# Softplus of the gates with tokens on partitions, and three feed-forward tiles split during the third branch's projection

## The chip, the cores and the metric

The kernel runs on one core of one Trainium2 chip. The metric is the device time of one execution in microseconds (us), taken as the median of several runs. The engines are TensorE (PE, matrix multiply; PEld is its weight load), VectorE (DVE), ScalarE (ACT), GpSimd (POOL) and SyncE (SP, which issues most DMAs).

## What is computed

Two layers of a hybrid decoder trunk on T = 288 tokens (256 of one prompt, 8 x 4 of eight decoding sequences), model width 1024, all in fp32. In each layer one projection feeds three mixers with four heads of width 128 each; their outputs are projected back, merged by sigmoid gates, and two layer norms follow, with a feed-forward block between them.

```
proj = einsum('btd,de->bte', x, w_in)
...
g = -exp(dn_A_log) * softplus(a_decay + dn_dt_bias)      # branch A, gated DeltaNet
gc = cumsum(g)                                           # in chunks
...
F = cumsum(log_sigmoid(m_f + ml_f_bias))                 # branch C, mLSTM
...
merged = g_a * (o_a @ w_br_a) + g_b * (o_b @ w_br_b) + g_c * (o_c @ w_br_c)
h = layer_norm(alpha * x + merged @ w_out, ln1_g, ln1_b)
ff = square(relu(h @ w_ff1)) @ w_ff2
out = layer_norm(alpha * h + ff, ln2_g, ln2_b)
```

Both `g` and `F` need a softplus (log_sigmoid(f) = -softplus(-f)) of four heads each, for every token: 8 x 288 numbers per layer.

## The kernel before, in words

Activations lie with channels on partitions and the 288 tokens in the free dimension. An fp32 product is made of three matmuls: the weights are split into `wh` (rounded) and `wl` (the rest), the activations into `XH` and `XL`, and `mm3` (L367 to L369) adds wh*XH, wh*XL and wl*XH. A full tile is 8 x 3 = 24 such matmuls of 128x288, and L498 is the same for tiles that fill gaps. `Stream.get` brings a weight tile: a 512 KB DMA on SP's queue into one of four `wr` buffers (L351), the cast to `wh` on ACT (L358), and the subtraction that gives `wl` on DVE (L360). With `get("B")` the two halves go to larger buffers, `bh` and `bl`, of a pool of 16, and so can be kept for longer.

A layer starts with the gates. Their projection is brought to 128 partitions by two small groups of matmuls, and ACT writes the biased gates `GT` (L626). Rows 32 to 35 are the forget gates of branch C, rows 64 to 67 the decay of branch A. Then the short convolutions of branch A (`conv_group`: ACT copies `CV` out of PSUM at L589 and L590, DVE builds `CO` at L604 and L607) go on beside the softplus, which works on all 128 partitions x 288 elements: U = GT*sgn (L643), E = exp(-|U|) on ACT (L645, L646), then a series in E/(2+E) on DVE (L648 to L659, with a RECIPROCAL at L649), U*sc (L660) and the running sum `CS` (scan, L662). From `CS` a chain of small operations on 4 partitions (L665 to L697) makes the running maximum and the row vectors `rc`, and at its end `drv` (L709 to L711) and `dr` (L714). PE's `dec` (L718), `colp` (L727) and `cols` (L737) take these up. The tiles of `rq`, `rk` and `rv` (branch B) are projected meanwhile; `rq` then goes through `rotary` (L570 to L572 on DVE).

Later in the layer, branch C's queries are scaled (`QL`, L1086), transposed on DVE (`Q`, L1090) and used by the matmuls `W` (L800). `ZG` (L542, L1022) gathers output gates.

After the mixers, `w_br_b`, `w_br_a` and `w_br_c` are applied in this order, in a loop over eight tiles `j` each; the merge into `mg` follows on DVE (L1301, L1302). The product with `w_out` (`wo`) feeds the generator `layer_norm`: per tile `yo` (L1343), sums `sd` and `sqs`; after the eighth tile the statistics `p` come back through PE, and a chain ACT, DVE (L1371 to L1380) makes `rstd`; `yo*rstd` (L1386) is split into `XH`, `XL` (L1388 to L1394), and the first feed-forward matmuls `f` (L375 to L377) begin. At the eighth `wo` tile (f = 8 of `AHEAD_FF`) the first five tiles of `w_ff1` are fetched with `get("B")`.

The build sets each engine's order from the dependencies and its own costs; `issue_after` in the source pins an instruction behind another one. All PSUM tiles come from two rings, `pm` (3) and `px` (5).

Of the kernel before, what the change touches and what calls it, by code (L numbers as in the profile page):

```python
# [9 lines left out]
F32 = mybir.dt.float32  # L10
# [13 lines left out]
GROUP = 3  # L24
# [226 lines left out]
def tile_trunk(ctx, tc, a):  # L251
# [36 lines left out]
    def R(name, dt=F32):  # L288
        return rp.tile([P, T], dt, tag="R", name=nm(name))
# [18 lines left out]
    for m_ in QM:  # L308
        G.memset(m_, 0.0)
    RB = cp.tile([P, T], F32R, name="RB")  # L310
# [8 lines left out]
    def C(n):  # L319
        o, s_ = CONST[n]  # L320
        return cst[:, o:o + s_]

    def VEC(l, n_, i, n=1):
        o = VECS[n_][0] + i
        return vec[:, l, o:o + n]
# [37 lines left out]

    def mm3(ps, hi, lo, xh, xl, start=True, stop=True):
        KT = len(xh)
        for k in range(KT):
            PE.matmul(ps, hi[:, k, :], xh[k], start=start and k == 0, stop=False)  # L367
            PE.matmul(ps, hi[:, k, :], xl[k], start=False, stop=False)  # L368
            PE.matmul(ps, lo[:, k, :], xh[k], start=False, stop=stop and k == KT - 1)  # L369
# [87 lines left out]
    for l in range(L):  # L457
# [168 lines left out]
        S.activation(GT, ps[:, :T], AF.Identity, bias=VEC(l, "gb", 0))  # L626

# [14 lines left out]
        U = R("U")  # L642
        V.tensor_scalar(U, GT, C("sgn"), None, op0=ALU.mult)  # L643
        E_ = R("E")
        S.activation(E_, U, AF.Abs)  # L645
        S.activation(E_, E_, AF.Exp, scale=-1.0)  # L646
        den = R("den")
# [3 lines left out]
        s2 = den  # L651
        V.tensor_tensor(s2, E_, E_, op=ALU.mult)
        pl = R("pl")
# [4 lines left out]
        V.tensor_scalar(U, U, 0.0, None, op0=ALU.max)  # L658
        V.scalar_tensor_tensor(U, pl, 2.0, U, op0=ALU.mult, op1=ALU.add)  # L659
        V.tensor_scalar(U, U, sc, None, op0=ALU.mult)  # L660
        CS = R("CS")
        V.tensor_tensor_scan(CS, C("rm"), U, 0.0, op0=ALU.mult, op1=ALU.add)  # L662
# [38 lines left out]
        rq = rotary(tproj("rq"))  # L701
# [572 lines left out]
        G.dma_start(a["o_m"][l], mo_[32:36, :])  # L1274

        MG_ = [h4(B("mg")) for _ in range(2)]
        for n_, (bi, wn) in enumerate(((1, "w_br_b"), (0, "w_br_a"), (2, "w_br_c"))):
# [14 lines left out]
            for j in range(8):  # L1292
                hi, lo = st.get()
                ps = PM("br")
                mm3(ps[:, :T], hi, lo, [OH[:, k, :] for k in range(4)], [OL[:, k, :] for k in range(4)])
                gt = TG[j // 4][:, j % 4, :]
# [139 lines left out]
        def prefetch_ff():  # L1436
            st = Stream([a["w_ff1"][l, i] for i in range(16)], 8)
            got = []

            def at(f):  # L1440
                n = AHEAD_FF[f]
                while len(got) < n:
                    got.append(st.get("B"))
                return got[:GROUP], (got[GROUP:], st)
            return at

# [82 lines left out]
```

## Time and profile before

| | before |
|---|---|
| median of 3 runs | 1219.05 us (1218.41 to 1221.0) |
| profiled execution, its own time | 1222.33 us |
| its span, first to last instruction | 1220.6 us |
| mean granted TensorE clock | 0.983 |
| busy: PE, PEld, DVE, ACT, POOL | 1178.3, 1146.9, 874.8, 639.1, 14.0 us |
| HBM read, written | 180.49 MB, 17.03 MB |

The profile gives one execution. Busy time is the time in which an engine had an instruction in work; "idle before" is the time an engine waited ahead of an instruction, with the one that released it. PEclk is the clock granted to TensorE, as a share of full speed (1.0 is 2.4 GHz, 0.5 is 1.2 GHz).

### The profile page before, as it was taken

The page shows a single profiled execution, that of the slowest core. Times are in us where ns is not written, and L with a number is a line of the kernel's source. Part 1 is how long each engine was busy: PE and PEld are TensorE (multiplying, and loading weights), DVE is VectorE, ACT ScalarE, POOL GpSimd, SP SyncE. Part 2 cuts the span into 40 slices and gives each one's busy share as a digit, 9 for nine tenths or more (in the row PEclk, how much of TensorE's full clock was granted, in tenths as well). Part 3 has the DMA queues.
Part 4 walks back from the last instruction along what each step waited for, and adds up shares of the span by engine and source line. Part 5 has one row for each costly group of instructions (what it writes and reads, how often), then busy time and mean ns, then how long its engine had stood idle before and what let it go on. Part 6 is the DMA issues. An engine that isn't in the chain of part 4 may idle for free.

```text
span 1220.6 us, 22885 instructions
## 1 busy us (share of the span) xinstructions
PE 1178.3 (97%) x9150; PEld 1146.9 (94%) x9150; DVE 874.8 (72%) x1655; ACT 639.1 (52%) x1162; POOL 14.0 (1%) x41
## 2 busy tenths in 40 slices
PE   8999999999999999999998998999999999999995
PEld 8899999999999899999998898999999989999995
DVE  5999856586668964566899995656866798545665
ACT  5745434883356653455584543349644566435542
POOL 1000000000000000000000000000000000000000
PEclk8999999999999999999999998999999999999998
DMA  8455635466655365555815354245666454555551
GB/s 304 128 157 134 232 91 164 136 243 207 222 155 171 97 185 169 168 162 161 257 40 179 123 187 143 96 139 213 229 200 193 146 172 133 162 170 163 166 156 39
DMA packets 69795, 201.15 MB, mean 165 GB/s; under 512 B 11688, under 2 KB 22232, under 8 KB 69560
## 3 DMA queue, kind: packets, MB, share of 16 engines
q1 hardware_dynamic: 68744, 197.51, 50.7%
q0 software_dynamic: 944, 2.17, 0.5%
q8 instruction: 72, 1.18, 0.4%
q14 instruction: 35, 0.29, 0.1%
HBM read 180.49 MB, written 17.03 MB: 162 GB/s over the span
## 4 chain that ended last, share of the span: by engine, by line
PE 81%; DVE 12%; ACT 3%; DMA 2%; issue 2%; SPq 0%; ACTq 0%; DVEq 0%
PE f L369 10%; PE f L368 10%; PE f L367 10%; PE pj L498 7%; PE pg L367 4%; PE pg L368 4%; PE pg L369 4%; PE pj L367 3%; PE pj L368 3%; PE pj L369 3%; DVE wl L360 3%; PE br L367 2%; PE br L368 2%; PE br L369 2%; DMA wr<-in_w_ff 2%
## 5 line engine op out<-in xcount | busy, mean ns | idle before, releaser
L358 ACT CAST wh<-wr 128x1024 fp32r<-128x1024 f32 x292 | 306.3, 1050 | 342.9 <-PE f L368 96.3
L360 DVE TENSOR_TENSOR wl<-wr,wh 128x1024 fp32r<-128x1024 f32 x292 | 356.1, 1223 | 173.6 <-ACT wh L358 173.0
L369 PE MATMUL f<-fh,wl 128*128 128x288 f32 x512 | 151.2, 295 | 0.0
L368 PE MATMUL f<-fl,wh 128*128 128x288 f32 x512 | 151.1, 295 | 0.0
L367 PE MATMUL f<-fh,wh 128*128 128x288 f32 x512 | 150.9, 295 | 0.0
L369 PE MATMUL f<-XH,wl 128*128 128x288 f32 x416 | 122.7, 295 | 0.7 <-DVE wl L360 0.7
L368 PE MATMUL f<-XL,wh 128*128 128x288 f32 x416 | 123.1, 296 | 0.0
L367 PE MATMUL f<-XH,wh 128*128 128x288 f32 x416 | 122.9, 296 | 0.0
L367 PE MATMUL pg<-XH,wh 128*128 128x288 f32 x384 | 114.2, 297 | 0.0
L368 PE MATMUL pg<-XL,wh 128*128 128x288 f32 x384 | 114.0, 297 | 0.0
L369 PE MATMUL pg<-XH,wl 128*128 128x288 f32 x384 | 113.4, 295 | 0.0
L369 PE MATMUL pj<-XH,wl 128*128 128x288 f32 x352 | 104.8, 300 | 3.4 <-DVE wl L360 3.4
L367 PE MATMUL pj<-XH,wh 128*128 128x288 f32 x352 | 106.1, 302 | 1.7 <-ACT CV L590 1.7
L368 PE MATMUL pj<-XL,wh 128*128 128x288 f32 x352 | 105.1, 299 | 0.0
L498 PE MATMUL pj<-XH,wh 128*128 128x288 f32 x320 | 98.2, 307 | 0.0
L498 PE MATMUL pj<-XH,wl 128*128 128x288 f32 x320 | 97.4, 305 | 0.3 <-DVE wl L360 0.3
L498 PE MATMUL pj<-XL,wh 128*128 128x288 f32 x320 | 97.0, 303 | 0.0
L367 PEld LDWEIGHTS f<-fh,wh 128*128 128x128 f32 x512 | 96.3, 188 | 0.2
L369 PEld LDWEIGHTS f<-fh,wl 128*128 128x128 f32 x512 | 96.2, 188 | 0.1
L368 PEld LDWEIGHTS f<-fl,wh 128*128 128x128 f32 x512 | 96.2, 188 | 0.1
L369 PEld LDWEIGHTS f<-XH,wl 128*128 128x128 f32 x416 | 78.5, 189 | 1.4 <-DVE wl L360 1.3
L367 PEld LDWEIGHTS f<-XH,wh 128*128 128x128 f32 x416 | 78.6, 189 | 0.0
(510 smaller groups left out, 2764.0 us busy)
## 6 DMA issues: line engine op xcount, KB each, us to landing
wr<-in_w_in SPq DMA_DIRECT2D x141, 512.0 KB
wr<-in_w_ff SPq DMA_DIRECT2D x128, 512.0 KB
wr<-in_w_out SPq DMA_DIRECT2D x16, 512.0 KB
S<-in_state_ml_C SPq DMA_DIRECT2D x8, 516.0 KB
S<-in_state_ret_R SPq DMA_DIRECT2D x8, 512.0 KB
out_s_R<-S SPq DMA_DIRECT2D x8, 512.0 KB
S<-in_state_dn_S SPq DMA_DIRECT2D x8, 512.0 KB
wr<-in_w_br_b SPq DMA_DIRECT2D x8, 512.0 KB
```

The costliest lines, as they stand in the source:

```text
L358: S.copy(hi[:, k, :], r[:, k, :])
L360: V.tensor_tensor(lo[:, k, :], r[:, k, :], hi[:, k, :].bitcast(F32), op=ALU.subtract)
L367: PE.matmul(ps, hi[:, k, :], xh[k], start=start and k == 0, stop=False)
L368: PE.matmul(ps, hi[:, k, :], xl[k], start=False, stop=False)
L369: PE.matmul(ps, lo[:, k, :], xh[k], start=False, stop=stop and k == KT - 1)
L498: ins = PE.matmul(self.ps[:, :T], self.w[i // 2][:, k, :], (xh, xl, xh)[i][k], start=self.k == 0, stop=self.k == 23)
```

## The change

Two edits, each in both layers.

**Softplus.** ACT now writes the sign-scaled gates U straight from PSUM, beside GT. Three PE transposes (`ut`) put the tokens on partitions, so that the eight gate rows that are needed become 3 x 2 x 4 = 24 elements on each of 128 partitions. The series runs on these 24 elements. Its last step writes into a zeroed tile `SPZ`, and three transposes (`sp`) bring the result back to 68 rows x 288. They are pinned behind the last matmul of `rq`, whose projection is now called ahead of them; U*sc and the scan work on 68 partitions.

**Feed-forward tiles.** The stream of `w_ff1` is made ahead of the merge loop, and three of its tiles are fetched in the third branch's loop, at j = 1, 3 and 5. Two are left for f = 8 of the layer norm.

```diff
--- before.py
+++ after.py
@@ -307,6 +307,8 @@
     QM = [cp.tile([P, H, T], F32, name=f"QM{i}") for i in range(2)]
     for m_ in QM:
         G.memset(m_, 0.0)
+    SPZ = cp.tile([P, 3, 68], F32, name="SPZ")
+    G.memset(SPZ, 0.0)
     RB = cp.tile([P, T], F32R, name="RB")
     V.memset(RB.bitcast(F32), 0.0)
     vec = cp.tile([P, L, VEC_W], F32, name="vec")
@@ -361,12 +363,14 @@
                 self.ready = [(hi[:, :, q:q + P], lo[:, :, q:q + P]) for q in range(0, sw, P)]
             return self.ready.pop(0)
 
+    mm_last = [None]
+
     def mm3(ps, hi, lo, xh, xl, start=True, stop=True):
         KT = len(xh)
         for k in range(KT):
             PE.matmul(ps, hi[:, k, :], xh[k], start=start and k == 0, stop=False)
             PE.matmul(ps, hi[:, k, :], xl[k], start=False, stop=False)
-            PE.matmul(ps, lo[:, k, :], xh[k], start=False, stop=stop and k == KT - 1)
+            mm_last[0] = PE.matmul(ps, lo[:, k, :], xh[k], start=False, stop=stop and k == KT - 1)
 
     def mm3_group(pss, tiles, xh, xl, ks=range(8)):
 
@@ -624,6 +628,9 @@
             PE.matmul(ps[32 * q:32 * q + 32, :T], C("gsel")[:, 4 * q:4 * q + 32], gp, start=True, stop=True,
                       tile_position=(0, 32 * q))
         S.activation(GT, ps[:, :T], AF.Identity, bias=VEC(l, "gb", 0))
+        sgb, U = K("sgb", 1), R("U")
+        V.tensor_tensor(sgb, VEC(l, "gb", 0), C("sgn"), op=ALU.mult)
+        S.activation(U, ps[:, :T], AF.Identity, bias=sgb, scale=C("sgn"))
 
         conv_group(1, "dk", None, dn_[:4])
         conv_group(2, "dv", st_dv, dn_[4:])
@@ -639,27 +646,35 @@
         G.memset(RS2, 0.0)
         S.activation(RS1[0:4], GT[0:4], AF.Tanh, scale=0.5)
         V.tensor_scalar(RS1[0:4], RS1[0:4], 0.5, 0.5, op0=ALU.mult, op1=ALU.add)
-        U = R("U")
-        V.tensor_scalar(U, GT, C("sgn"), None, op0=ALU.mult)
-        E_ = R("E")
-        S.activation(E_, U, AF.Abs)
+
+        ps = PX("ut")
+        for i, t0 in enumerate((0, P, T - P)):
+            PE.transpose(ps[:, i * P:(i + 1) * P], U[:, t0:t0 + P], ident)
+        u = ps[:, :3 * P].rearrange("p (c y x) -> p c y x", c=3, x=32)[:, :, 1:3, 0:4]
+        g3 = (lambda n_: K(n_, 3, 2, 4))
+        E_, den, pl, s2 = g3("gE"), g3("gden"), g3("gpl"), g3("gs2")
+        S.activation(E_, u, AF.Abs)
         S.activation(E_, E_, AF.Exp, scale=-1.0)
-        den = R("den")
         V.tensor_scalar(den, E_, 2.0, None, op0=ALU.add)
         V.reciprocal(den, den)
         V.tensor_tensor(E_, E_, den, op=ALU.mult)
-        s2 = den
         V.tensor_tensor(s2, E_, E_, op=ALU.mult)
-        pl = R("pl")
         V.tensor_scalar(pl, s2, 1.0 / 13, None, op0=ALU.mult)
         for d_ in (11, 9, 7, 5, 3):
             V.scalar_tensor_tensor(pl, pl, 1.0 / d_, s2, op0=ALU.add, op1=ALU.mult)
         V.scalar_tensor_tensor(pl, pl, 1.0, E_, op0=ALU.add, op1=ALU.mult)
-        V.tensor_scalar(U, U, 0.0, None, op0=ALU.max)
-        V.scalar_tensor_tensor(U, pl, 2.0, U, op0=ALU.mult, op1=ALU.add)
-        V.tensor_scalar(U, U, sc, None, op0=ALU.mult)
+        V.tensor_scalar(den, u, 0.0, None, op0=ALU.max)
+        for y in range(2):
+            V.scalar_tensor_tensor(SPZ[:, :, 32 + 32 * y:36 + 32 * y], pl[:, :, y, :], 2.0, den[:, :, y, :], op0=ALU.mult,
+                                   op1=ALU.add)
+        rq = tproj("rq")
+        ps = PX("sp")
+        with tc.issue_after(mm_last[0].ins):
+            for i, t0 in ((2, T - P), (1, P), (0, 0)):
+                PE.transpose(ps[:68, t0:t0 + P], SPZ[:, i, :], ident)
+        V.tensor_scalar(U[:68], ps[:68, :T], sc[:68], None, op0=ALU.mult)
         CS = R("CS")
-        V.tensor_tensor_scan(CS, C("rm"), U, 0.0, op0=ALU.mult, op1=ALU.add)
+        V.tensor_tensor_scan(CS[:68], C("rm")[:68], U[:68], 0.0, op0=ALU.mult, op1=ALU.add)
         Fr, gc = CS[32:36], CS[64:68]
         IT = R("IT")
         V.tensor_copy(IT[32:36], GT[96:100])
@@ -698,7 +713,7 @@
         for q in (0, 64):
             S.copy(RB[q:q + 4], rc_[q:q + 4])
             V.tensor_tensor(RB[q + 32:q + 36], rc_[q:q + 4], RB[q:q + 4].bitcast(F32), op=ALU.subtract)
-        rq = rotary(tproj("rq"))
+        rq = rotary(rq)
         rk, fill = tproj("rk", fill=True)
         rv, fill.then = tproj("rv", fill=True)
         fill.done = lambda: rotary(rk)
@@ -1272,6 +1287,15 @@
         fin_m = finish(OM, dn, MG, None, 2, 8, 9)
 
         G.dma_start(a["o_m"][l], mo_[32:36, :])
+        ff_st, ff_got = Stream([a["w_ff1"][l, i] for i in range(16)], 8), []
+
+        def prefetch_ff():
+            def at(f):
+                while len(ff_got) < AHEAD_FF[f]:
+                    ff_got.append(ff_st.get("B"))
+                return ff_got[:GROUP], (ff_got[GROUP:], ff_st)
+            return at
+
 
         MG_ = [h4(B("mg")) for _ in range(2)]
         for n_, (bi, wn) in enumerate(((1, "w_br_b"), (0, "w_br_a"), (2, "w_br_c"))):
@@ -1293,6 +1317,8 @@
                 hi, lo = st.get()
                 ps = PM("br")
                 mm3(ps[:, :T], hi, lo, [OH[:, k, :] for k in range(4)], [OL[:, k, :] for k in range(4)])
+                if n_ == 2 and j in (1, 3, 5):
+                    ff_got.append(ff_st.get("B"))
                 gt = TG[j // 4][:, j % 4, :]
                 mg = MG_[j // 4][:, j % 4, :]
                 if n_ == 0:
@@ -1433,17 +1459,6 @@
                                        op1=ALU.subtract)
             return [XF[:, f, :] for f in range(8)]
 
-        def prefetch_ff():
-            st = Stream([a["w_ff1"][l, i] for i in range(16)], 8)
-            got = []
-
-            def at(f):
-                n = AHEAD_FF[f]
-                while len(got) < n:
-                    got.append(st.get("B"))
-                return got[:GROUP], (got[GROUP:], st)
-            return at
-
         YO = [h4(B("yo")) for _ in range(2)]
         pre, (pre2, ff_st), ff_after = layer_norm(out_tiles(), YO, base_x, shift_x, "ln1_g", "ln1_b", prefetch_ff)
 
```

The order moves at three places on which the prediction rests. The numbers behind names count tiles; they differ between the two kernels for the same tile.

DVE, layer 0, around the `wl` of the first `rq` tile (before: `wl_714`; after: `wl_693`). `CO` is the convolution; `U`, `den`, `E`, `pl` are the softplus. Before:

```order
38 L604 SCALAR_TENSOR_TENSOR CO_626<-CV_487,vec,CO_626 128x312
39 L649 RECIPROCAL den_664<-den_664 128x288
40 L604 SCALAR_TENSOR_TENSOR CO_626<-CV_487,vec,CO_626 128x312 x2
41 L650 TENSOR_TENSOR E_661<-E_661,den_664 128x288
42 L604 SCALAR_TENSOR_TENSOR CO_626<-CV_487,vec,CO_626 128x312 x4
43 L652 TENSOR_TENSOR den_664<-E_661 128x288
44 L604 SCALAR_TENSOR_TENSOR CO_626<-CV_487,vec,CO_626 128x312
45 L654 TENSOR_SCALAR pl_669<-den_664 128x288
46 L360 TENSOR_TENSOR wl_714<-wr_711,wh_713 128x1024
```

After:

```order
33 L362 TENSOR_TENSOR wl_598<-wr_595,wh_597 128x1024
34 L608 SCALAR_TENSOR_TENSOR CO_632<-CV_493,vec,CO_632 128x312
35 L611 SCALAR_TENSOR_TENSOR CO_471<-CV_394,CO_471 128x1260
36 L608 SCALAR_TENSOR_TENSOR CO_632<-CV_493,vec,CO_632 128x312
37 L362 TENSOR_TENSOR wl_693<-wr_690,wh_692 128x1024
38 L608 SCALAR_TENSOR_TENSOR CO_632<-CV_493,vec,CO_632 128x312 x3
39 L362 TENSOR_TENSOR wl_725<-wr_722,wh_724 128x1024
40 L608 SCALAR_TENSOR_TENSOR CO_632<-CV_493,vec,CO_632 128x312 x4
41 L362 TENSOR_TENSOR wl_757<-wr_754,wh_756 128x1024
42 L608 SCALAR_TENSOR_TENSOR CO_632<-CV_493,vec,CO_632 128x312
43 L658 TENSOR_SCALAR gden_670<-gE_669 128x24
```

The `wl` of the first `rq` tile now stands ahead of all softplus operations but the 128x1 `sgb`, and two more of its tiles follow it there; the softplus comes behind the third.

DVE, layer 1, around `QL` and `Q` of branch C, for which PE's `W` waits. `ZG<-ZG,pj` takes a finished fill tile out of PSUM, `ZG<-tp,ZG` the result of eight transposes that PE does behind the last fill tile; `rst`, `rsu`, `fr` are 128x1. Before:

```order
1042 L391 TENSOR_SCALAR rsu_1334_8820<-rst_1333_8811 128x1
1043 L392 TENSOR_TENSOR rsu_1334_8820<-rsu_1334_8820,rst_1333_8811 128x1
1044 L542 SCALAR_TENSOR_TENSOR ZG_8680<-ZG_8680,pj_8765 128x288
1045 L1022 TENSOR_TENSOR ZG_8434<-tp_8792,ZG_8434 128x4x128
1046 L1022 TENSOR_TENSOR ZG_8434<-tp_8798,ZG_8434 128x4x128
1047 L393 SCALAR_TENSOR_TENSOR fr_1331_8809<-rsu_1334_8820,rsy_1332_8810 128x1
1048 L1086 TENSOR_TENSOR QL_8826<-qc_8318,cst 128x1152
1049 L1004 TENSOR_SCALAR fr_1331_8809<-fr_1331_8809 128x1
1050 L1090 STREAM_TRANSPOSE Q_1336_8828<-QL_8826 128x1152
```

After:

```order
1028 L546 SCALAR_TENSOR_TENSOR ZG_8706<-ZG_8706,pj_8714 128x288
1029 L996 SCALAR_TENSOR_TENSOR S_8559<-S_8559,up_8746 128x2x128
1030 L390 TENSOR_SCALAR rst_1341_8837<-rst_1341_8837 128x1
1031 L362 TENSOR_TENSOR wl_8865<-wr_8862,wh_8864 128x1024
1032 L391 TENSOR_TENSOR rsy_1340_8836<-rsy_1340_8836,rst_1341_8837 128x1
1033 L1101 TENSOR_TENSOR QL_8852<-qc_8344,cst 128x1152
1034 L546 SCALAR_TENSOR_TENSOR ZG_8706<-ZG_8706,pj_8758 128x288
1035 L392 TENSOR_TENSOR rst_1341_8837<-rsy_1340_8836 128x1
1036 L1105 STREAM_TRANSPOSE Q_1344_8854<-QL_8852 128x1152
```

`pj_8765` before is the last fill tile ahead of W; `pj_8758` after is the second last. QL and Q stand behind the last tile and the transposes before, and around the second-last tile after.

ACT, layer 0, at the end of the first layer norm. `wh<-wr` casts a weight tile that a DMA brings; `Cb<-sqs` and `Cb<-Cb` are the logarithm and exponential for `rstd`, and `sqt`, `XH<-yo` belong to the last tiles of `wo`. Before:

```order
337 L1345 ACTIVATE sqt_4730<-yo_4416 128x288
338 L333 ACTIVATE XH_4493<-yo_4416,vec 128x288
339 L358 CAST wh_4921<-wr_4919 128x1024
340 L1371 ACTIVATE Cb_4417<-p_726_4694 128x288
341 L358 CAST wh_5032<-wr_5030 128x1024
342 L358 CAST wh_5068<-wr_5066 128x1024
343 L1376 ACTIVATE Cb_4417<-sqs_4419 128x288
344 L1377 ACTIVATE Cb_4417<-Cb_4417 128x288
345 L1388 ACTIVATE XH_4493<-yo_4415,vec 128x288 x4
```

After:

```order
335 L360 CAST wh_4935<-wr_4933 128x1024
336 L1371 ACTIVATE sqt_4722<-yo_4448 128x288
337 L335 ACTIVATE XH_4525<-yo_4448,vec 128x288
338 L360 CAST wh_5046<-wr_5044 128x1024
339 L360 CAST wh_5082<-wr_5080 128x1024
340 L1371 ACTIVATE sqt_4762<-yo_4448 128x288
341 L335 ACTIVATE XH_4525<-yo_4448,vec 128x288
342 L1397 ACTIVATE Cb_4449<-p_739_4726 128x288
343 L1402 ACTIVATE Cb_4449<-sqs_4451 128x288
344 L1403 ACTIVATE Cb_4449<-Cb_4449 128x288
345 L1414 ACTIVATE XH_4525<-yo_4447,vec 128x288 x4
```

Two casts stood between the statistics `Cb<-p` and the logarithm; now all casts stand ahead of the statistics. On DVE, five `bl` splits stood among the operations on the last `wo` tiles, and two stand there now.

## Rows read from the trace of the kernel before

**Rows 1.** The page: busy time by engine.
```profile
PE 1178.3 (97%) x9150; PEld 1146.9 (94%) x9150; DVE 874.8 (72%) x1655; ACT 639.1 (52%) x1162; POOL 14.0 (1%) x41
```

**Rows 2.** PE's waits: who waited for whom, us in total, times, longest.
```profile
PE dec L718 <- DVE dr L714: 4.6, 2, 2.4
```

**Rows 3.** Windows: length, busy PE, PEld, DVE, ACT, POOL (instructions), PEclk, DMA share, GB/s.
```profile
40.00:50.00 10.00, 10.00 (x78) 10.00 (x77) 9.86 (x17) 8.26 (x19) 0.54 (x1) 1.00 0.57 184
50.00:60.00 10.00, 8.09 (x47) 7.63 (x46) 10.00 (x19) 4.50 (x10) 0.54 (x1) 0.83 0.29 81
650.00:660.00 10.00, 7.91 (x59) 7.68 (x59) 10.00 (x14) 4.19 (x7) 0.00 (x0) 1.00 0.49 161
740.00:750.00 10.00, 5.76 (x43) 5.56 (x42) 9.06 (x24) 2.70 (x4) 0.00 (x0) 0.92 0.72 262
344.00:356.00 12.00, 12.00 (x92) 12.00 (x92) 7.21 (x12) 5.81 (x11) 0.00 (x0) 1.00 0.56 158
356.00:368.00 12.00, 12.00 (x92) 11.94 (x91) 11.73 (x23) 5.82 (x10) 0.00 (x0) 1.00 0.43 146
```

**Rows 4.** Windows of stretches at half clock, the first and the last of six.
```profile
55.44:58.85 3.41, 3.41 (x17) 3.41 (x16) 3.41 (x6) 1.25 (x1) 0.00 (x0) 0.51 0.39 145
...
1007.90:1011.40 3.50, 3.50 (x17) 3.50 (x16) 3.50 (x11) 2.44 (x6) 0.00 (x0) 0.52 0.07 28
```

**Rows 5.** Timeline of PE, layer 0, first `rq` tile: start, us, instruction, [idle before].
```profile
52.66 0.40 PE L367 MATMUL pj<-XH,wh 128*128 128x288 f32 x1 [0.83 <-ACT CV L590]
...
54.27 0.40 PE L369 MATMUL pj<-XH,wl 128*128 128x288 f32 x1 [1.08 <-DVE wl L360]
```

**Rows 6.** DVE's groups by form, the whole execution: us in total, mean ns, idle before.
```profile
L649 DVE RECIPROCAL den<-den 128x288 f32<-128x288 f32 x2 | 3.9, 1946 | 0.0
L386 DVE TENSOR_SCALAR rst<-rst 128x9 f32<-128x9 f32 x4 | 0.7, 171 | 0.1
```

**Rows 7.** DVE's groups by form, 40 to 90 us (layer 0's gates).
```profile
L656 DVE SCALAR_TENSOR_TENSOR pl<-pl,den 128x288 f32<-128x288 f32 x5 | 2.2, 447 | 0.0
...
L571 DVE TENSOR_TENSOR rot<-rot,cst 128x1152 f32<-128x1152 f32 x1 | 1.4, 1352 | 0.0
```

**Rows 8.** Timeline of DVE, layer 0: the scan and the end of its chain.
```profile
64.93 0.76 DVE L662 TENSOR_TENSOR_SCAN CS<-cst,U 128x288 f32<-128x288 f32 x1
...
73.04 0.16 DVE L711 TENSOR_TENSOR drv<-vec,M 4x8 f32<-4x8 f32 x1
```

**Rows 9.** Timeline of PE and DVE, layer 1, ahead of `W`.
```profile
744.05 1.03 PE L1012 MATMUL tp<-ident,OR 128*128 128x128 f32 x8
745.15 1.28 DVE L1022 TENSOR_TENSOR ZG<-tp,ZG 128x512 f32<-128x512 f32 x2
746.41 1.35 DVE L1086 TENSOR_TENSOR QL<-qc,cst 128x1152 f32<-128x1152 f32 x1
747.80 1.38 DVE L1090 STREAM_TRANSPOSE Q<-QL 128x1152 f32<-128x1152 f32 x1
...
749.32 0.55 PE L800 MATMUL W<-Q,E 128*128 128x128 f32 x1 [4.24 <-DVE Q L1090]
```

**Rows 10.** Timeline of all engines, layer 0, end of the first layer norm.
```profile
396.39 1.22 DVE L360 TENSOR_TENSOR bl<-wr,bh 128x1024 fp32r<-128x1024 f32 x1
...
397.49 1.05 ACT L358 CAST wh<-wr 128x1024 fp32r<-128x1024 f32 x1 [0.49 <-DMA wr<-in_w_ff]
...
400.32 1.05 ACT L358 CAST wh<-wr 128x1024 fp32r<-128x1024 f32 x1 [1.78 <-DMA wr<-in_w_ff]
401.28 0.43 ACT L1376 ACTIVATE Cb<-sqs 128x288 f32<-128x288 f32 x1
...
405.02 0.82 DVE L1386 TENSOR_TENSOR yo<-yo,rstd 128x288 f32<-128x288 f32 x2
...
406.19 0.40 PE L375 MATMUL f<-XH,bh 128*128 128x288 f32 x1 [2.70 <-DVE XF L1392]
```

**Rows 11.** Timeline of PE, layer 1, first feed-forward matmuls.
```profile
1007.58 0.66 PE L375 MATMUL f<-XH,bh 128*128 128x288 f32 x2 [2.04 <-ACT XH L1388]
```

## Prediction, made before the changed kernel was run

> **What bounds the kernel now.** I read the busy times first: PE works 1178.3 of 1220.6 us and the next engine, DVE, 874.8 [rows 1]. So a change that takes no matmul away can only win the 42 us in which PE is idle, and the time that it loses at half clock. The mean granted clock of 0.983 says that the second is about half as large: 1.7% of the span is 20 us of lost clock.
>
> Next I read the list of PE's waits and looked each one up in the windows and the timeline. A full stretch holds 78 matmuls in 10 us, a pitch of 0.128 us (the stretch from 40 us, [rows 3]). At the head of `rq` in layer 0 the count is 47, and DVE is busy for all of the 10 us: 31 x 0.128 = 4.0 us are lost [rows 3]. PE stood there for a PSUM slot that ACT emptied late and then 1.08 us for the `wl` of the first `rq` tile [rows 5]; that `wl` was late because DVE took softplus and convolution operations ahead of it. In layer 1 the same place has 59 of 78, 2.4 us lost, again with DVE at 10.00 of 10 [rows 3]. Later PE waits 2.4 and 2.2 us for `dr`, the end of the gates' chain [rows 2], 4.24 us for `Q` in layer 1 [rows 9], 2.70 us at the end of the first layer norm in layer 0 and 2.04 us in layer 1 [rows 10, 11].
>
> What such a wait costs is more than its length. Behind five of these waits, and behind the pair at `rq`, the clock stands at about 0.5 for 3.4 to 3.9 us; PE had stood idle for 1 to 4 us just before [rows 4, 5, 9 to 11]. Seventeen matmuls fit in 3.41 us there, where 26 would at the full pitch: 1.2 us by the count, 1.7 by the clock. I take 1.5 us for each.
>
> **Part 1, the softplus.** On DVE it removes 14 operations of 128x288 per layer: the RECIPROCAL of 1.95 us [rows 6], nine with two tensor inputs at 0.45 us [rows 7], and four with one input, at two thirds of that: some 7 us. It adds a 128x1 product and 14 operations of 128x24 or less. None of that size stands in the trace. The bounds are 0.17 us (128x9, [rows 6]) and 0.45 us (128x288, [rows 7]); 24 elements are nearest to 9, so I take 0.18. For the small RECIPROCAL the bounds are 0.17 and 1.95; a twelfth of the long one's time above 0.17 gives 0.15 more, so 0.32. Together 14 x 0.18 + 0.32 = 2.8 us. DVE saves some 4.5 us (bounds 0.5 and 5) where it was busy without a break. Thirty-two times as many elements cost only 2.6 times as much [rows 6, 7]: that is why twelve times less work does not shrink twelvefold.
>
> ACT gets one more 128x288 write (about 0.45 us) and loses nearly as much on the two shorter ones; it is busy 4.5 of 10 us there [rows 3]. POOL's one memset lies at the program's start. Neither counts. PE gets six transposes per layer. Eight of PE's `tp` transposes take 1.03 us [rows 9], so these cost 0.8 us, all of it on the path.
>
> What matters more is the order. The three `wl` that `rq` needs first now stand ahead of the softplus on DVE, so the loss at the head of `rq` should go: 4.0 us in layer 0, 2.4 in layer 1.
>
> The end of the gates' chain I expect to gain nothing. The result now comes back through `sp`, which is held behind the 96 matmuls of `rq`. In layer 0 PE starts `rq` at 51.9 us after three transposes, ends it 96 x 0.129 = 12.4 us later at 64.3, and does `sp` until 64.7. U*sc and one `wl` (1.22 us, [rows 10]) stand ahead of the scan, which starts at about 66.4, where it was 64.93. From scan to `drv` took 8.1 us [rows 8], with one `wl` in it that is no longer there: 6.9, so 73.3. Behind `drv` DVE now does two of the rotary's long operations (1.35 us each, [rows 7]) and RB before `dr`: `dec` can go at 77.2, against 75.9 before. PE has 75 fill matmuls between `sp` and `dec` (it had 41 between `rq` and `dec`), and arrives at 64.7 + 75 x 0.129 = 74.4. So it waits 2.8 us where it waited 2.4, and the half clock stays. The balance at `dec` is 34 more matmuls done, 4.4 us, for 1.3 us later: **-3.1 us in layer 0**, transposes included. In layer 1 `dr` stood behind these two operations already. There I take the 2.4 us, less 0.8 for transposes, plus 0.4 because the chain has one `wl` less in it: **-2.0 us**.
>
> **The move of Q.** In layer 1 `QL` waited in DVE's order behind the last fill tile's `ZG` and two operations on transposes (1.28 us) that PE itself had only just made [rows 9]; then QL 1.35 and Q 1.38 followed, and W could go 4.24 us late. Now QL and Q stand around the second-last tile's `ZG`. That tile ends 24 x 0.129 = 3.1 us before the last one, and the eight transposes take 1.03: W is wanted 4.1 us behind the second-last tile, and 0.45 + 1.38 us with two 0.15 operations is what stands behind it on DVE, some 2.1 us. The wait of 4.24 and the 1.5 of half clock go, and I leave 0.5 for a late `ZG`: **-5.2 us**. In layer 0 no such wait exists to win.
>
> **Part 2, the feed-forward tiles.** At the end of the layer norm the logarithm stood on ACT behind a cast that waited 1.78 us for its DMA [rows 10], and three of the `bl` splits (1.22 us each) that stood between DVE's last operations are gone. Now the logarithm stands behind no cast, and `rstd`'s chain has no `wl` in its middle. The first `yo*rstd` was at 405.02; without 1.78 us of ACT's wait, one cast of 1.05 and one `wl` of 1.22 it comes 3 to 4 us sooner. PE had stood since 403.5 (406.19 less 2.70): the wait goes but for a few tenths. It is worth 2.70 + 1.5 = 4.2 us in layer 0 and 2.04 + 1.5 = 3.5 in layer 1. Of each I take four fifths, since other casts and splits move too: **-3.4 and -2.8 us**.
>
> The three tiles have to be split in the third branch's stretch instead. There DVE is busy 7.21 of 12 us and then 11.73 of 12, with PE full in both [rows 3]. Three splits are 3.7 us, three casts 3.2; the first stretch has 4.8 us free on DVE, the second none. The tiles come at j = 1, 3, 5, so two of them hit the full stretch, but `wl` buffers run a tile ahead. I cost it at nothing; the cover is the idle DVE before 356 us. If the cover is gone, each tile costs PE its 1.22 us: 3.7 us per layer plus 1.5 of clock. The DMAs move 146 GB/s of the 262 that another stretch shows [rows 3]; 1.5 MB more in 12 us makes 277, just at that mark.
>
> **The sum.** -3.1 - 2.0 - 5.2 - 3.4 - 2.8 = -16.5 us. Of this some 5.4 us are clock: 1.5 at `rq`, 1.5 at W, and four fifths of 1.5 at each layer norm. The profiled execution took 1222.33 us (its span is 1220.6), which makes 1205.8. It lies 3.3 us above the median of the runs, so against the median: 1219.05 - 16.5 = **1202.5 us**.
>
> On the clock the rows and a rule differ. The rows show a whole execution at 0.983, with a stretch at 0.51 behind each long wait [rows 4]. The Trainium skill (TensorE: Matmul & The Clock Gate, section What's actually happening) says that the loss while the clock comes up is under 1% of a typical kernel and should not be fitted for a model. By that rule the 5.4 us would be left out, and the estimate would be 1207.9 us. This trace loses 1.7%, in stretches that each have their wait, so I keep them.
>
> **The rivals.**
> 1. *Only the layer norm pays.* The wait moves: `dr` comes later by the rotary's 2.7 us in full, the gates' gain is spent at `dec`, and `Q` lands late again. For it speaks that DVE stays near full in these stretches; against it that `rq`'s `wl` and Q demonstrably move ahead in the order. It gives -6.2 and about -1: 1212.
> 2. *All of the waits go*, those for `dr` too, because DVE has 4.5 us less to do. Then the terms reach their full size (4.0 + 2.4 - 1.6 + 5.7 + 4.2 + 3.5 = 18.2) and 2.4 + 2.2 + 2 x 1.5 = 7.6 us come on top: 1193. Against it speaks `sp`'s place behind `rq`.
> 3. *Slower: the three early tiles starve the third branch.* A weight tile's DMA that came late held ACT, and casts followed each other at 2.8 us (397.49 to 400.32, [rows 10]). If the three tiles delay the tiles of `w_br_c` and `w_out` behind them on SP's queue and in the four `wr` buffers by that much each, PE loses 8.5 us and 1.5 to 3 of clock per layer, 21 in all: 1219.05 - 16.5 + 21 = 1224. It decides from 8.3 us per layer on. Against it: the DMA engines are 0.43 busy there [rows 3].
> 4. *No change.* PE has the same matmuls and twelve transposes more, 1.6 us; if each wait that goes comes back at the next place where DVE is full, the time is 1219 to 1221. Against it: behind the `rq` stretch, the W and the layer norm, the DVE has free time before PE next needs it. The Trainium skill (Perfetto Trace Analysis, section Identifying the Most-Contended Engine) says to optimize the engine with the highest occupancy first; by that rule, relieving DVE at 72% would win nothing, and this rival would be the forecast. The windows do not bear it out: in them DVE is the full engine and PE the one with gaps.
>
> **How the numbers follow.** Chances: the forecast 0.62, rival 1 0.17, rival 2 0.09, rival 3 0.06, rival 4 0.06. The range reaches from rival 2 to just past rival 1: 1193 to 1213, and leaves out rivals 3 and 4 and the tails. A change of 0.2% (2.4 us) is about what can be told from none. Faster by more: 0.88; within: 0.06; slower: 0.06.
>
> **What would show it.** PE's waits should no longer hold `W` on `Q`, `f` on `XF` or `XH`, or `pj` on `wl` at the head of `rq`; `dec` on `dr` should stay near 2 to 3 us in both layers. The count of matmuls in the first 10 us of `rq` should be above 70 in layer 0, and the mean clock rise towards 0.99. The small operations should take under 0.2 us, the RECIPROCAL under 0.4. It is wrong if W still waits, if PE waits in the third branch's loop or at `w_out`, or if `wo` waits grow by more than 3 us.

## The result, and the profile after

The changed kernel takes 1201.09 us (median of 4 runs, 1199.93 to 1203.68); the kernel before took 1218.73 us beside it. The ratio is 0.9861, with a 95% interval of 0.9842 to 0.9881: 17.6 us faster, against 16.5 forecast. Run again later beside other kernels it took 1200.16 us against 1219.86, a ratio of 0.9837 (0.9816 to 0.9859). The profiled execution took 1201.68 us, with a span of 1199.9 us.

The page's busy times, after:

```profile
PE 1170.1 (98%) x9162; PEld 1139.7 (95%) x9162; DVE 866.4 (72%) x1657; ACT 638.7 (53%) x1164; POOL 14.2 (1%) x42
```

PE's idle time fell from 42.3 us [rows 1] to 1199.9 - 1170.1 = 29.8. The mean granted clock rose from 0.983 to 0.992: lost clock went from 1.7% of 1220.6 us, 20.7, to 0.8% of 1199.9, 9.6. So 12.5 us of the gain in this pair are waits, and the rest comes out of the 11 us of clock. But the profiled execution of before had less clock than most: in the 17 runs of before beside the experiments below the median of the mean clock is 0.987, against 0.992 in the four runs of the changed kernel, which is about 6 us of clock and not 11. DVE's busy time fell by only 8.4 us, 4.2 per layer, where 4.5 was reckoned.

The list of PE's waits, after (who waited for whom, us in total, times, longest):

```profile
PE dec L733 <- DVE dr L729: 2.8, 2, 1.4
PE pj L502 <- ACT wh L360: 2.4, 2, 1.3
PE wo L371 <- DVE yo L1369: 1.7, 2, 0.9
...
PE cols L752 <- DVE rep L751: 1.2, 2, 0.7
```

No wait of `W` for `Q`, of `f` for `XF` or `XH`, or of `pj` for `wl` is left in the list, which answers to [rows 9 to 11] and [rows 5]. The largest that are left, `dec` and the `pj` ahead of it, stand at the end of the gates' chain.

The windows, after (length, busy PE, PEld, DVE, ACT, POOL with instructions, PEclk, DMA share, GB/s): the head of `rq` in layer 0, the end of the gates, `rq` in layer 1 from its head on (two that overlap), and two of the third branch.

```profile
50.00:60.00 10.00, 10.00 (x78) 10.00 (x77) 9.42 (x25) 6.49 (x15) 0.54 (x1) 1.00 0.57 164
70.00:80.00 10.00, 6.84 (x43) 6.04 (x43) 9.76 (x27) 3.97 (x8) 0.52 (x1) 0.86 0.03 10
640.00:650.00 10.00, 10.00 (x78) 10.00 (x77) 9.02 (x22) 6.79 (x13) 0.54 (x1) 1.00 0.53 166
645.00:655.00 10.00, 10.00 (x78) 9.98 (x77) 7.45 (x15) 5.50 (x8) 0.00 (x0) 1.00 0.51 157
344.00:356.00 12.00, 12.00 (x92) 12.00 (x92) 9.05 (x14) 7.39 (x11) 0.00 (x0) 1.00 0.87 268
356.00:368.00 12.00, 11.60 (x86) 11.13 (x85) 10.07 (x22) 5.19 (x10) 0.00 (x0) 1.00 0.45 143
```

At `rq` the counts are 78 where they were 47 and 59 [rows 3]. In the third branch the DMAs now move 268 GB/s where they moved 158, DVE is busy 9.05 of 12 us where it was 7.21, and PE loses 0.4 us in the second window, where `wo` begins.

DVE's groups by form, 45 to 66 us (layer 0's softplus):

```profile
L664 DVE SCALAR_TENSOR_TENSOR gpl<-gpl,gs 128x24 f32<-128x24 f32 x5 | 0.9, 180 | 0.1
...
L675 DVE TENSOR_SCALAR U<-sp,sc 68x288 f32<-68x288 f32 x1 | 0.5, 517 | 1.3 <-PE sp L674 1.3
L659 DVE RECIPROCAL gden<-gden 128x24 f32<-128x24 f32 x1 | 0.3, 296 | 0.0
```

A 24-element operation takes 0.18 us, as reckoned from the 9-element row [rows 6], and the RECIPROCAL 0.296, against 0.32. U*sc, which now reads the PSUM tile `sp`, takes 0.52 us; before it took 0.37 on 128x288, and I had left it at that. (That is four fifths of the 0.45 of a two-input operation, not the two thirds that I took for its kind; no term of the sum hangs on it.)

Where the time went is best read by laying the two traces side by side at the same matmul. Start of the first matmul of each kind, before and after, in the two profiled executions:

```
                         before    after   difference
last pj ahead of rq       51.00    49.77      -1.2
dec, layer 0              75.90    76.43      +0.5
sc (branch B's scores)   109.71   105.98      -3.7
W, layer 0               149.79   146.19      -3.6
wo, layer 0              363.95   360.37      -3.6
f, layer 0               406.19   400.52      -5.7
layer norm 2, layer 0    603.93   595.75      -8.2
sc, layer 1              707.65   695.58     -12.1
X (behind W), layer 1    762.00   745.31     -16.7
wo, layer 1              966.46   949.85     -16.6
f, layer 1              1007.58   989.35     -18.2
end of the span         1220.6   1199.9      -20.7
```

By stretches: ahead of `rq` -1.2, gates of layer 0 -2.5, first layer norm of layer 0 -4.6 with what follows it, gates of layer 1 -3.9, W -4.6, first layer norm of layer 1 -4.1 with the end of the program. The sum is the spans' 20.7 (rounding aside), 3 us more than the medians' difference: the profiled execution of before stood 3.3 us above the median of its runs, as the prediction said.

Three of these figures are not what they seem. Up to the last `pj` ahead of `rq` PE does the same in the same order in both kernels, so the first -1.2 does not come from the change; the clock at the program's start was lower for longer in the profiled execution of before. Its window from 5 to 16 us, and that of after:

```profile
5.00:16.00 11.00, 8.87 (x40) 8.11 (x41) 7.28 (x12) 6.93 (x11) 0.00 (x0) 0.69 1.03 356
5.00:16.00 11.00, 9.23 (x51) 8.46 (x51) 7.18 (x12) 6.91 (x12) 0.00 (x0) 0.84 1.03 358
```

And in layer 1 the two kernels do not do the same work between `sc` and W. The windows from the first `sc` to the first W, before and after:

```profile
707.65:749.32 41.67, 37.34 (x325) 34.12 (x324) 37.30 (x108) 18.52 (x31) 0.56 (x1) 0.99 0.62 215
695.58:735.48 39.90, 39.40 (x344) 36.61 (x343) 36.40 (x106) 17.21 (x32) 0.56 (x1) 1.00 0.59 197
```

Counted by their starts, 18 more matmuls of 128x288 stand there after the change, and 18 fewer ahead of `sc`: at 0.129 us each that is 2.3 us of work moved from the gates to W. With equal work the gates of layer 1 gained 3.9 - 2.3 = 1.6 us and W 4.6 + 2.3 = 6.9 us.

### The profile page after: what moved, and what is told of

Same layout as the page of the kernel before. It is cut to its first block, busy times and chain, and to the rows that moved or that the text cites. A ratio compares the mean times of both kernels' runs of the same rounds, so it can differ in the third digit from the quotient of the medians.

```text
span 1199.9 us, 22910 instructions
## 1 busy us (share of the span) xinstructions
PE 1170.1 (98%) x9162; PEld 1139.7 (95%) x9162; DVE 866.4 (72%) x1657; ACT 638.7 (53%) x1164; POOL 14.2 (1%) x42
## 4 chain that ended last, share of the span: by engine, by line
PE 89%; DVE 7%; ACT 1%; DMA 1%; issue 1%; SPq 0%; ACTq 0%; DVEq 0%
PE f L372 10%; PE f L371 10%; PE f L373 10%; PE pj L502 9%; PE pg L371 4%; PE pg L372 4%; PE pg L373 4%; PE pj L371 4%; PE pj L372 4%; PE pj L373 4%; PE br L371 2%; PE br L372 2%; PE br L373 2%; DVE wl L362 2%; PE tp L413 1%
```

## The experiments

Ten further kernels ran. The first four were compared with 17 runs of before (median 1219.47 us), the others with 17 more each time (1219.87 and 1219.86).

**The softplus edit alone.** The changed kernel without the early fetches:

```diff
-                if n_ == 2 and j in (1, 3, 5):
-                    ff_got.append(ff_st.get("B"))
```

> The softplus edit alone; all five feed-forward tiles are fetched at the end of the first layer norm as before. Theory: the two edits act in different stretches, and the place of Q and QL on DVE comes with this edit. From the two traces: 3.6 us gained by W of layer 0, 3.9 between the two layers' ends of the gates, 4.6 at W of layer 1, so about 12 us below before (some 1207 us), PE's waits for Q gone, and the 2.7 and 2.0 us waits for the first feed-forward matmuls still there. Rival: the time at W belongs to the other edit: then about 1212 us and W still waits 4 us for Q.

It took 1209.71 us, a ratio of 0.9925 (0.9903 to 0.9948): 9.8 us, where the two traces had made 12 expected. The first line of PE's list of waits:

```profile
PE f L379 <- ACT XH L1412: 4.4, 2, 2.4
```

The waits for the feed-forward's first matmuls are back, and in the list W has none. So what W gained belongs to this edit, which does not touch `Q` in the source: the build placed it elsewhere.

**The feed-forward edit alone**, on the kernel before:

```diff
+                if n_ == 2 and j in (1, 3, 5):
+                    ff_got.append(ff_st.get("B"))
```

> The feed-forward edit alone on the kernel before. Theory: the waits at the first feed-forward matmuls and the half clock behind them go in both layers, 4.6 + 4.0 us by the traces, so about 1210 to 1212 us; W still waits about 4 us for Q, the head of rq still loses 4.0 and 2.4 us. Rival: the three early splits cost PE time in the third branch (waits of wo or br above 1 us more per layer): then 1214 us or more.

It took 1211.90 us, a ratio of 0.9943 (0.9924 to 0.9962): 7.6 us. The two parts add up: 9.8 + 7.6 = 17.4, against 17.6 for both. Its list of waits begins with the three of before that are not the layer norm's:

```profile
PE dec L718 <- DVE dr L714: 4.6, 2, 2.4
PE W L800 <- DVE Q L1090: 4.2, 1, 4.2
PE pj L369 <- DVE wl L360: 3.4, 3, 2.1
```

**Q back behind the last fill tile.** The changed kernel, in layer 1:

```diff
-        V.tensor_tensor(QL...
+        with tc.issue_after(zg_last[0].ins) if l else nullcontext():
+            V.tensor_tensor(QL...
```

> The changed kernel, with QL of layer 1 pinned on DVE behind the last fill tile's ZG. Theory: the place of QL and Q on DVE is what the W term is made of: W waits again 2.5 to 4 us and the half clock comes back with it, so 3 to 5 us over the changed kernel (1204 to 1206 us). Rival: what W gained is lost or won elsewhere anyway: within 1 us of the changed kernel.

It took 1209.06 us, a ratio of 0.9923 (0.9899 to 0.9947): 8 us over the changed kernel, more than either theory said. The line of PE's waits, and then DVE ahead of W:

```profile
PE W L815 <- DVE Q L1106: 5.1, 1, 5.1
```

```profile
736.18 1.28 DVE L1037 TENSOR_TENSOR ZG<-tp,ZG 128x512 f32<-128x512 f32 x2
737.38 1.35 DVE L1102 TENSOR_TENSOR QL<-qc,cst 128x1152 f32<-128x1152 f32 x1
738.65 1.22 DVE L362 TENSOR_TENSOR wl<-wr,wh 128x1024 fp32r<-128x1024 f32 x1
739.78 1.37 DVE L1106 STREAM_TRANSPOSE Q<-QL 128x1152 f32<-128x1152 f32 x1
```

The pin let a `wl` of 1.22 us slip in between QL and Q, so the wait is longer than the 4.24 us of before [rows 9]. And around and behind it the clock stands at half for 6.8 us (740.2 to 747.0 us, granted clock 0.50), in which PE is busy for 5.70, so 2.9 us are lost: with the wait 8.0 us, which is what was measured. The expectation had both too small, the clock above all. In the changed kernel the same operations stand here, and W starts where the transposes leave off (PE and DVE, after):

```profile
732.65 1.37 DVE L1105 STREAM_TRANSPOSE Q<-QL 128x1152 f32<-128x1152 f32 x1
...
734.61 1.03 PE L1027 MATMUL tp<-ident,OR 128*128 128x128 f32 x8
...
735.48 1.06 PE L815 MATMUL W<-Q,E 128*128 128x128 f32 x8
```

**The order without the small operations.** The kernel before, softplus on 128x288, pinned behind the third `wl` of `rq`:

```diff
+        rq = tproj("rq")
+        with tc.issue_after(wl_all[n0 + 2].ins):
+            U = R("U")
...
```

> The kernel before with the softplus left as it is (128 x 288 elements), but its DVE operations pinned behind the wl of the third rq tile: the order of the change without its smaller operations. Theory: the loss at the head of rq is a matter of order and goes (over 70 matmuls in the first 10 us of rq), but the long operations make the chain to dr late, so dec waits longer and about half of the gates' gain is lost: 1213 to 1217 us. Rival: order is all there is to it: dec waits no longer than before, and the time is that of the softplus edit alone, about 1207 to 1209 us.

It took 1224.43 us, a ratio of 1.0053 (1.0034 to 1.0073): 5 us slower than before, so both theories missed. A window at `rq`, and DVE's and PE's timeline:

```profile
50.00:60.00 10.00, 10.00 (x78) 10.00 (x77) 9.40 (x15) 7.73 (x17) 0.54 (x1) 1.00 0.64 177
```

```profile
71.01 0.76 DVE L667 TENSOR_TENSOR_SCAN CS<-cst,U 128x288 f32<-128x288 f32 x1
...
82.14 0.16 DVE L716 TENSOR_TENSOR drv<-vec,M 4x8 f32<-4x8 f32 x1
...
83.15 0.61 PE L500 MATMUL pj<-XH,wh 128*128 128x288 f32 x1 [4.94 <-ACT rk L555]
```

The loss at `rq` is gone: 78 matmuls, as in the changed kernel. But the scan comes at 71.0 us, where the changed kernel has it at 65.3 and before at 64.9 [rows 8], and from scan to `drv` it takes 11.1 us instead of 8.1, because the build put rq's three rotary operations into the chain. PE stands 4.9 us. So order alone wins the head of `rq`, and in this kernel the end of the chain pays more than that: counted from the last `pj` ahead of `rq`, `sc` of layer 0 starts 2.5 us later than before. The rest of the loss lies elsewhere. W now waits in both layers (5.9 us in all), where before it waited in layer 1 alone [rows 9]. So the run does not show what the short operations are worth by themselves: their length, the rotary's place and Q's place are not separated.

**What is left at dec.** Two runs moved the chain. The first pinned the rotary behind `dr`:

```diff
+        with tc.issue_after(dr_ins.ins):
+            rq = rotary(rq)
```

> The changed kernel with rq's rotary operations on DVE pinned behind dr. Theory: dr comes 2.5 us sooner after drv, but the build now puts dec 10 matmuls sooner on PE as well, 1.3 us, so PE still waits for dr for about 1 us and the time is 0 to 2 us under the changed kernel (1199 to 1201 us). Rival: the two rotary operations are the whole of what is left at dec: no wait for dr, no half clock behind it, 5 to 7 us under (1194 to 1196 us).

It took 1213.40 us, a ratio of 0.9952 (0.9931 to 0.9972), 12 us over the changed kernel: both theories missed. The start of its list:

```profile
PE W L815 <- DVE Q L1105: 8.5, 2, 4.2
PE dec L733 <- DVE dr L726: 5.9, 2, 3.1
```

A pin at `dr` moved `Q` behind the fill tiles in both layers, some 70 us later in the program. And `dec` stood 10 matmuls sooner on PE, and its wait grew from 2.8 us to 5.9.

The second put `sp` behind the third tile of `rq`:

```diff
-        with tc.issue_after(mm_last[0].ins):
+            if j == 2:
+                with tc.issue_after(mm_last[0].ins):
...
+        rq = tproj("rq", then=back)
```

> The changed kernel with the transposes sp behind the third tile of rq instead of the fourth; the build also puts dr ahead of the rotary and dec 33 matmuls sooner. Theory: the chain is 3 us earlier, but so is PE at dec, so the wait stays at 2 to 3 us: within 2 us of the changed kernel (1199 to 1203 us). Rival: sp behind all of rq is what holds the chain: the waits at dec vanish and 5 to 8 us are won (1193 to 1196 us).

It took 1198.88 us, a ratio of 0.9826 (0.9802 to 0.9849). The theory held: `sp` is done at 59.4 us instead of 63.5, and `dec` starts at 71.03 us instead of 76.43, but with 34 matmuls fewer ahead of it, and PE waits for `dr` longer than before the change (4.6 us, [rows 2]):

```profile
PE dec L741 <- DVE dr L737: 5.8, 2, 3.0
```

Q's place stayed good here. Run again beside the changed kernel:

> The kernel with sp behind the third rq tile once more, beside the changed kernel: 1 to 2.5 us under it, as the traces' 1.5 us at the end of the gates say.

It took 1198.64 us (0.9827, 0.9803 to 0.9850) and the changed kernel, in the same hour:

> The changed kernel once more, beside the others of this list: 0.9861 of before within its interval, 1200 to 1204 us.

1200.16 us (0.9837, 0.9816 to 0.9859; runs from 1200.03 to 1200.67). The version with the earlier `sp` was 2.2 us (across two jobs) and 1.5 us (side by side) under the changed kernel; the intervals overlap, so a gain is not shown.

**More matmuls between sp and dec**, on top of the earlier `sp`:

```diff
-FILL_C = (3, 3, 2, 3)
+FILL_C = (19, 3, 2, 3)
```

> As the run with sp behind the third rq tile, and 19 instead of 3 units of fill (57 matmuls) asked for ahead of dec, so that 80 matmuls stand between sp and dec. Theory: the wait at dec is set by the number of matmuls between sp and dec against a chain of about 13 us from sp to dr: with 80 of 0.129 us, 10.3 us, and some 2 us of waits for weights, PE waits under 1 us, no half clock follows, and the time is 4 to 8 us under the changed kernel (1193 to 1197 us). Rival: the fill is missing later, and waits come up behind the gates: no gain.

It took 1220.93 us (1.0018, 1.0000 to 1.0036). Its list of waits begins:

```profile
PE W L823 <- DVE fr L397: 10.9, 2, 5.4
PE tp L413 <- DVE cd L800: 4.0, 2, 2.2
PE cols L760 <- DVE rep L759: 3.0, 2, 1.5
```

`dec` is gone from the list, as said, but the kernel is 20 us slower by the median, and 15 us in the profiled execution: mainly by Q's place again (`fr` stands right behind Q on DVE and ends 0.05 us after it), and by the operations on columns behind the rotary. Two more pins, on Q and on the rotary, were to show whether that was all:

```diff
+        with tc.issue_after(hb_ins.ins):
+            rq = rotary(rq)
...
+        with tc.issue_after(q_ins.ins):
+            fill(0, 23)
+            fin_rp()
```

> As the run with 57 matmuls asked for ahead of dec, with two more pins on DVE: rq's rotary stands behind the operations that turn dec's, colp's and cols' results into columns, and the third z tile's ZG and the end of the retention branch stand behind Q. Theory: that run lost its gain to W (10.9 us of waits) and to the long rotary operations ahead of the column copies (7.0 us at tp and cols), and not to the missing fill: with both moved it comes to 1192 to 1198 us, no wait at dec, under 2 us at W in all. Rival: matmuls missing later make PE wait in other places: 1203 us or more.

> As the run before it in this list, with 75 instead of 57 matmuls asked for ahead of dec. Theory: nothing is left to win at dec, and 18 matmuls more there are missing behind the gates: within 3 us of that run, above it rather than below.

They took 1209.80 us (0.9914, 0.9894 to 0.9934) and 1225.55 us (1.0043, 1.0024 to 1.0061). Neither theory held; the first one's rival had the number, 1203 us or more, but PE waits for Q and not for want of matmuls. Of the first the list begins:

```profile
PE W L823 <- DVE Q L1110: 9.9, 2, 4.9
PE pj L502 <- DVE ZG L546: 2.8, 2, 1.4
```

The waits at `tp` and `cols` fell from 7.0 us to 1.1, so the rotary was most likely their cause; but my pin held the ZG tiles back instead of bringing Q forward, so W still waits. Even so, branch B's scores in layer 0 began at 106.58 us, not before the 105.98 of the changed kernel, with no wait at `dec`: what was won there was spent behind it. Whether a kernel with all three waits gone exists is left open. In the second, W waits 7.8 us, and new waits come up behind the gates, first of them:

```profile
PE stk L940 <- ACT sx L936: 5.2, 4, 2.4
```

What else its 16 us over the first are made of was not taken apart.

**All five tiles early.**

```diff
-                if n_ == 2 and j in (1, 3, 5):
+                if n_ == 2 and j in (1, 2, 3, 5, 6):
```

> The changed kernel with all five feed-forward tiles fetched in the third branch's loop (j = 1, 2, 3, 5, 6) and none at the end of the layer norm. Theory: DVE and the weight buffers cover three splits there, not five: PE waits 1 to 2 us more per layer at br or wo, and the layer norm has no wait left to win: 1202 to 1206 us. Rival: the cover is large enough: 1199 to 1201 us, with the waits as in the changed kernel.

It took 1208.17 us (0.9903, 0.9881 to 0.9925), 7 us over the changed kernel. A wait at the head of `w_out`, and a window of the third branch:

```profile
PE wo L371 <- DVE tg L1327: 3.7, 2, 1.9
```

```profile
356.00:368.00 12.00, 10.13 (x64) 9.81 (x62) 10.23 (x22) 4.89 (x10) 0.00 (x0) 0.86 0.63 184
```

DVE is busy for all of the 6 us from 356 and reaches the merge late (`tg`, L1327), PE stands 1.9 us in each layer, and half clock follows: 64 matmuls where the changed kernel has 86. This is the third rival's place at a smaller price: DVE, not the DMAs, runs out first, for in the 12 us ahead the DMAs moved 299 GB/s and PE was full.

## Why the prediction was right

**The bound.** PE's waits and the clock behind them were what there was to win, and both fell as said. The Trainium skill (Perfetto Trace Analysis, section Identifying the Most-Contended Engine) says to optimize the engine with the highest occupancy first, which here is PE. That relieving DVE at 72% would then win nothing was my inference, and it does not hold: the 17.6 us were won by relieving DVE in the stretches in which PE waited for it. The fourth rival falls. So does the first, since W's wait went and the gates kept a gain, the second, since `dec` still waits, and the third, since PE stays full in the third branch but for 0.4 us.

**The sum, and some luck in it.** I read the terms from the profiled execution of before, added them to -16.5, and took them from the median. Like for like, the terms stand against the 20.7 us of the profiled pair, or 19.5 without the 1.2 us at the program's start. So they were 3 us too small together. That the medians differ by 17.6, so near to the forecast, is luck in part: the run that I read the prices from had more half clock than most. The terms, forecast and traced (with equal work), one by one:

**Gates of layer 0, -3.1 forecast, -2.5 in the trace** (-2.2 in the run with this edit alone). The head of `rq` came out as said, at the full count. At the end I forecast 2.8 us of waiting for `dr` and half clock behind it. PE after, layer 0:

```profile
74.65 0.40 PE L502 MATMUL pj<-XH,wh 128*128 128x288 f32 x1 [1.34 <-ACT wh L360]
76.43 0.43 PE L733 MATMUL dec<-dr,ones 128*128 128x64 f32 x2 [1.38 <-DVE dr L729]
...
78.42 0.47 PE L752 MATMUL cols<-ident,rep 128*128 128x128 f32 x1 [0.45 <-DVE rep L751]
```

`dec` waited 1.38 us, less than the 2 to 3 that I had named as a sign; with the two waits beside it the sum is 1.34 + 1.38 + 0.45 = 3.2 us. The first I had not foreseen: a weight tile's cast stands on ACT behind the two of RB, which wait for the chain. The half clock came as forecast (0.51 from 77.2 to 80.7 us). So the sum of the waits holds, but not its parts.

**Gates of layer 1, -2.0 forecast, -1.6 in the trace.** The 2.4 us that one window shows [rows 3] went, and so did two waits of 0.84 and 0.24 us ahead of 650 us that I had not counted; PE is busy for all of the 15 us from 640, as the windows above show. New waits took part of it back: 0.77 us at 630.07, and 1.06 for `wh` and 0.72 at `cols` around `dec`.

**W, -5.2 forecast, -6.9 in the trace with equal work.** The mechanism is shown by the undoing run. This is the term most mis-sized, and the reason is a misreading: I took 1.5 us of clock behind each wait, from stretches of 3.4 to 3.9 us at half clock, but at W the stretch is twice as long:

```profile
748.40:755.20 6.80, 5.88 (x26) 5.91 (x27) 2.25 (x4) 0.58 (x1) 0.00 (x0) 0.50 0.25 77
```

PE is busy for 5.88 us of it, so 2.9 us are lost by the clock and not 1.5; with the wait of 4.24 that makes 7.2. That Q's place hangs on the build's order and on nothing that the edit computes is shown by three runs in which edits elsewhere (the pin behind `dr`, the pin behind `rq`'s third `wl`, more fill ahead of `dec`) left W waiting in both layers.

**Layer norms, -3.4 and -2.8 forecast, -4.6 and -4.1 in the traces; 7.6 us measured for both with the edit alone.** The full size, 4.2 and 3.5, would have been nearer than the four fifths that I took, and the stretch of 3.4 us at half clock behind each lost 1.7 us, not 1.5. The chain after, layer 0, DVE, ACT and PE:

```profile
395.61 0.45 ACT L1402 ACTIVATE Cb<-sqs 128x288 f32<-128x288 f32 x1 [2.43 <-DVE sqs L1400]
...
399.19 0.82 DVE L1412 TENSOR_TENSOR yo<-yo,rstd 128x288 f32<-128x288 f32 x2
...
400.52 0.43 PE L379 MATMUL f<-XH,bh 128*128 128x288 f32 x2
```

The logarithm now waits for DVE and not behind a cast that waits for a DMA [rows 10], and PE does not stand ahead of `f`. The three early splits cost PE 0.4 us in layer 0, in the window from 356 us above, against nothing forecast; in layer 1 PE is busy for all of the 24 us from 933, which answer to these windows.

**The clock.** I took the 20 us of lost clock as there to be won. But the last of the half clock, from 1209.2 us on, stands where PE has no instruction left, and so does that of after, from 1190.0 us on: 5.7 of the 20.7 us and 5.0 of the 9.6 cost nothing. I kept 5.4 us of clock in the sum; the profiled pair won about 10, and the medians of the runs' mean clocks, 0.987 and 0.992, make about 6. So the clock had to be in the sum: without it the forecast would have been 1207.9 us, 6.8 over what came. The sentence of the Trainium skill that I set against it (TensorE: Matmul & The Clock Gate, section What's actually happening) is about the loss while the clock comes up, and there the trace agrees: at the program's start, in the window from 5 to 16 us above, a mean of 0.69 makes 3.4 us of lost clock, 0.3% of 1220.6. It says nothing against a loss that each wait brings anew; to leave out the 5.4 us by it was my reading of it.

## What to carry to other kernels

Where the bound engine is 97% busy, look at the short stretches in which another engine is full and it is not; waits of 2.0 and 2.7 us there were worth 4.1 and 4.6 with the clock behind them. Moving the wanted operation ahead on the full engine wins the wait, but watch the end of the chain that it is moved ahead of: in the one run that moved the order without shortening that chain, the loss came back there. And where a build sets the order, read the order of the whole program after every edit: here the place of one transposition, some 70 us behind the edit, stood behind W's waits in six kernels, 2.9 to 5.4 us each time, with half clock to follow. When two traces are laid side by side, count the work between the marks too; here 18 matmuls had changed places, and made one term look too large and another too small.

## What the runs showed of the hardware that was not expected

The same wait does not always bring half clock. The kernel before and the one with the feed-forward edit alone are the same up to the third branch, and both wait 2.44 us at `dec` in layer 0. Their windows from 75 to 80 us, before and then the other:

```profile
75.00:80.00 5.00, 4.10 (x20) 4.11 (x21) 4.67 (x10) 1.20 (x2) 0.00 (x0) 0.66 0.73 208
```

```profile
75.00:80.00 5.00, 4.67 (x37) 4.67 (x38) 5.00 (x10) 1.35 (x2) 0.00 (x0) 1.00 0.79 220
```

One runs at a mean of 0.66, the other at full clock, and does 17 matmuls more (some four of them because its `dec` stands 0.57 us sooner). Behind W the stretch was longer in one than in the other, too (the 6.82 us from W's first matmul, before and then the other):

```profile
749.32:756.14 6.82, 6.82 (x34) 6.82 (x35) 1.85 (x3) 0.62 (x2) 0.00 (x0) 0.57 0.25 77
```

```profile
740.32:747.14 6.82, 6.82 (x45) 6.82 (x46) 1.86 (x3) 1.17 (x2) 0.00 (x0) 0.78 0.22 77
```

This also moves the time of the runs of one and the same kernel. Before ran from 1213.52 to 1221.89 us in 17 runs. Each run's mean granted clock is on record beside its time: the three shortest, up to 1213.97 us, had 0.991 to 0.992, the three longest, from 1221.18 us, 0.984 to 0.985. Seven thousandths of 1220 us are 8.5 us, about the whole of the spread. So nearly all of the spread of the kernel before goes with the clock; what decides in a given run whether it falls behind a wait is not shown. The changed kernel, with fewer such waits, ran from 1199.93 to 1203.68 us in its eight runs. But waits alone do not foretell the spread: the kernel with Q back behind the last fill tile kept within 2.1 us in six runs.
